# Turning O, K, Q and the softmax weights of the first layer by 32x32 transposes on VectorE and a round trip through DRAM

## The chip, the core and the metric

The kernel runs on one core of a Trainium2 chip. The core's engines are TensorE (PE, with its weight loads PEld), VectorE (DVE), ScalarE (ACT), GpSimd (POOL) and SyncE (SP); transfers are carried by 16 DMA engines and are issued from the queues of SP, ACT and POOL. The metric is the device time of one execution in microseconds; lower is better.

## What is computed

Two layers of a hybrid block work on 256 tokens (x) and 256 context tokens (ctx), with 1024 features. Each layer projects the normed tokens by one wide matrix, runs three branches (A: an mLSTM over 4 heads; B: differential attention over 8 heads, two per group; C: a Fourier mix), gates them and merges them by matrix products. The second layer produces x alone. Branch B and the merge, which the change touches:

```python
def attend(q, k, v, lam):
    s = jnp.einsum('bhmqd,bhmkd->bhmqk', q, k, preferred_element_type=jnp.float32) * (B_QK ** -0.5)
    p = jax.nn.softmax(s, axis=-1)
    w = p[:, :, 0] - lam * p[:, :, 1]
    return jnp.einsum('bhqk,bhkv->bhqv', w.astype(v.dtype), v)

def diffattn_out(o, subln_w, lam_init):
    return (rmsnorm(o, subln_w) * (1.0 - lam_init)).transpose(0, 2, 1, 3).reshape(bsz, n, B_WIDTH)
...
    y_b = diffattn_out(o_b, subln_w, lam_init) * jax.nn.silu(bz)
...
    y = g_a * (y_a @ w_a_out) + g_b * (y_b @ w_b_out) + g_c * (y_c @ w_c_out)
    return y @ w_out
```

## The kernel before

All products are made at float32 accuracy from fp32r halves: a matrix is split into a high part (a rounding copy on ScalarE) and a low part (a subtraction on VectorE), and `three` (line 591 on) issues three matmuls for each product. The main stream is a chain of such matmuls into banks named pm. Weights come in pieces of 512 rows by 256 columns: SP loads `raw` (4 buffers), ACT and DVE split it into `wh` and `wl` (3 buffers each), and TensorE uses a piece for 24 or more main matmuls.

Beside the main stream run side generators: `a_side`, `b_side`, `c_side` and a few more. Each is a Python generator that emits a few instructions and then yields the time at which its next step may be emitted. A planner, the class `Clocks`, books every instruction that is emitted with an estimated cost, and `tick` lets up to 5 side generators emit steps between two main matmuls when the planner's TensorE clock has reached the time that they yielded. So the planner's costs set the order of the instructions on every engine, and each engine then runs its own list strictly in order, held back by semaphores alone. A transfer that POOL issues is booked with 1040 ns of POOL, its bytes at 290 GB/s on one queue, and 2000 ns until it is seen; `when` adds 400 ns (READY_NS).

The order of the first layer's units is ORDER0: A0 to A3 are the mLSTM heads, B0 to B3 the attention groups (two heads each), C0 to C3 the Fourier groups, then the merges M0 (branch A), M2 (C), M1 (B) and the output W0. M1 comes last; with AHEAD its four gate products run first, then the side work of branch B is drained, then the products with B's result start. When M1 starts, two generators for the next adaLN rows start too; they load w_ada in pieces of 512 KB by 24 transfers on POOL's queue (tiles `adaw`).

In `b_side` (line 964 on) the tokens lie on the partitions. For each head TensorE turns K and Q by `nc.tensor.transpose` (`transpose`, line 234) into a side bank `ps`, four 128x128 blocks each, and ACT and DVE split them into kT and qT. Then come 8 items for each group (two heads times four blocks of queries): the score matmuls, the softmax (`softmax`), the turning of its weighted difference `Pt` on TensorE into `ps` (`w_transpose`: 2 blocks for the context queries, 4 for the others), its split into `W`, and the product with V (`pv`). An item's weights are turned LAG = 3 items after its scores. At the end O is normed, turned by TensorE (8 blocks for each group), and multiplied into the gate `Gb`.

Tiles of up to 4128 bytes for each partition come from one pool `g` with NGEN = 28 slots, taken in turn: a new tile waits until the readers of the one 28 before it are done.

The trace names the helper's line: L232 is a matmul, L236 a TensorE transpose, L161 anything of the other engines.

Of the kernel before, what the change touches and what calls it, by code (L numbers as in the profile page):

```python
# [27 lines left out]
NGEN = 28  # L28
# [13 lines left out]
ORDER1 = "A0 B0 A1 B1 A2 A3 C0 B2 B3 M0 C1 C2 C3 M1 M2 W0"  # L42
AHEAD = ((0, 1, 1), (1, 1, 0))
# [47 lines left out]
class Clocks:  # L91
    """When each engine gets to what is emitted, estimated, to place the side work among the main products."""
# [5 lines left out]
    def book(self, engine, outs, ins, cost, tail):  # L98
        """an instruction of engine: names of tiles written and read, time held, time until the result is seen"""
# [16 lines left out]
    def rotate(self, tag, bufs, name):  # L116
        """the tile called name takes the place of the one bufs before it"""
# [9 lines left out]
class Paced:  # L127
    """An engine whose instructions are booked as they are emitted."""
# [38 lines left out]
def hybrid_kernel(ctx: ExitStack, tc: tile.TileContext, t):  # L167
# [18 lines left out]
    def when(*tiles, banks=1):  # L186
        """the time at which the tiles are written and side banks are free"""
# [17 lines left out]
    def gen_pair(shape, name):  # L205
        """hi and lo parts, in one slot where they fit"""
# [39 lines left out]
    # ------------------------------------------------------------- constants  # L246
# [73 lines left out]
    def rstd_of(ss, n, shape):  # L320
        """(ss / n + eps) ** -0.5 on GpSimd, in place; returns the time at which it is done"""
# [4 lines left out]
    # ------------------------------------------------------------- per-layer small parameters  # L326
# [46 lines left out]
    def ada_rows(l, piece, dma):  # L373
        """w_ada of 512 columns"""
# [8 lines left out]
    def ada_mm(raws, brow, dst):  # L383
        """sc @ w_ada + b_ada: partitions 32 g + stream hold four partial sums"""
# [13 lines left out]
    def ada_finish(l, pc, ks=slice(0, 8)):  # L398
        """pc: shift and scale of some blocks of features"""
# [9 lines left out]
    def ada_gen(l, pieces):  # L409
        """shift and scale columns (pieces 0..3) as a side generator"""  # L410
# [34 lines left out]
    # ------------------------------------------------------------- norm -> feature-major h  # L445
# [3 lines left out]
    def norm_stats(tiles):  # L449
        """normalized copies of some token tiles"""  # L450
# [10 lines left out]
    def norm_apply(l, i, src, base):  # L461
        """src: the normalized transposed blocks base .. base + 3 of token tile i; returns the closing step"""
# [23 lines left out]
    # ------------------------------------------------------------- weight pieces  # L486
# [74 lines left out]
    def fm_chunk(rhs, evac, ntok, bank=ps_main, step=4):  # L561
        """two 128-column blocks of W, feature-major: out[block][128 cols, tokens]"""
# [24 lines left out]
    def tm_chunk(lhs, tiles, evac, single=False, step=4):  # L587
        """256 columns of W, token-major: out[pair][128 tokens, 2, 256]"""
# [24 lines left out]
    # ------------------------------------------------------------- side machinery  # L613
# [4 lines left out]
    def launch(g):  # L618
        rec = {"g": g, "due": 0.0, "done": False}
        side.append(rec)  # L620
        return rec
# [8 lines left out]
    def tick():  # L630
        pe0 = clocks["pe"]
        for rec in list(side[:ACTIVE]):
# [12 lines left out]

    def hrhs(t0, n):
# [7 lines left out]
    # ============================================================= one layer  # L654
    def layer(l, P):
# [8 lines left out]
        def packed(name, i):  # L664
            """[128, 2, NTOK], two of them in a slot where they fit"""
# [6 lines left out]
        # ---------- branch A: gates  # L672
        def gates_side():
            """kind x head i of the gate preactivations: from column 32 x + i, token-major, to a partition"""
# [71 lines left out]
        # ---------- branch A: heads  # L746
# [72 lines left out]
        def a_side(h):  # L819
# [97 lines left out]
            for dh in range(2):  # L917
# [9 lines left out]
        # ---------- branch B  # L927
# [58 lines left out]
        def b_side(g):  # L986
# [25 lines left out]

            def qk_transpose(X, nt, n, name):
                ps = ps_side()
                for i in range(nt):
                    transpose(ps[:, 128 * i:128 * i + 128], X[:, i, 128 * hd:128 * hd + 128], ident)
                T = gen([128, 2, n], F32R, name)
# [6 lines left out]
            def softmax(hd, i, p2, n):  # L1024
                """the weighted difference of both maps, short of the first one's 1 / sum"""
# [8 lines left out]
                for m_ in range(2):  # L1034
# [12 lines left out]
            def w_transpose(Pt, n):  # L1047
                ps = ps_side()
                for k in range(n // 128):
                    transpose(ps[:, 128 * k:128 * k + 128], Pt[:, 0, 128 * k:128 * k + 128], ident)  # L1050
                W = gen([128, 2, 512], F32R, "W")
# [18 lines left out]
            for it in items + [None] * LAG:  # L1070
                cur = None
                if it is not None and it[1] == 0:
                    hd = it[0]
                    kT = qk_transpose(K, 4, 512, "kT")
# [8 lines left out]
                if it is not None:  # L1083
# [13 lines left out]
                    pend.append((hd, i, Pt, at, n, ri[:, 0:1]))  # L1097
# [10 lines left out]
            for hd in range(2):  # L1108
# [8 lines left out]
        # ---------- branch C  # L1117
        def c_proj(g):
# [3 lines left out]
            def evu(a, pr, ps):  # L1122
                """sums and differences of features d and d + 128"""
# [64 lines left out]
        # ---------- merge  # L1188
        yacc = {}

        def merge(recs, ahead, key, first, final):
            ys = {}

            def split_y(q):
                ys[q] = gen_pair([128, 2, NTOK], "y")
# [300 lines left out]
```

## Time and profile before

| | |
|---|---|
| median of 3 runs | 1522.9 us (1522.81 to 1523.61) |
| span of the profiled execution, first to last instruction | 1521.1 us |
| PE busy | 1499.1 us (99%) |
| PEld busy | 1350.8 us (89%) |
| DVE busy | 971.5 us (64%) |
| ACT busy | 735.0 us (48%) |
| POOL busy | 145.7 us (10%) |
| granted TensorE clock, mean | 1.000 |

The page gives no other time of the profiled execution than its span, which is 1.8 us under the median of the runs. Busy time of TensorE counts pipelined matmuls from start to modelled end, so what a matmul costs is read from the distance between the starts of two that follow each other. The first layer's branch B lies between 350 and 800 us.

### The profile page before, as it was taken

How to read it: one execution, taken by the hardware profiler on the slowest of the kernel's cores; microseconds unless marked ns; L12 is line 12 of the kernel's file. 1: busy time of each engine (PE TensorE's matmuls, PEld its weight loads, DVE VectorE, ACT ScalarE, POOL GpSimd, SP SyncE). 2: the span in 40 equal slices, each digit the busy share in tenths (PEclk: the TensorE clock that was granted, in tenths of full speed). 3: DMA queues.
4: the chain of work that ended last, by engine and by line, in shares of the span. 5: the costliest groups of instructions: out<-in, count | busy, mean ns of one | idle time of the engine just before them, and what ended most of it. 6: DMA issues, size and time to landing. Idle time of an engine off the chain costs nothing.

```text
span 1521.1 us, 25867 instructions
## 1 busy us (share of the span) xinstructions
PE 1499.1 (99%) x10410; PEld 1350.8 (89%) x10410; DVE 971.5 (64%) x1833; ACT 735.0 (48%) x1384; POOL 145.7 (10%) x193
## 2 busy tenths in 40 slices
PE   6999999999999999999999999999999999999999
PEld 4888889999998987897786789999999999999998
DVE  3447666677677586436664367677687666977765
ACT  4443556544544545334432235545557554656443
POOL 4001000020100010001024001001020011000200
PEclk9999999999999999999999999999999999999999
DMA  9524333332222222223249337544344523545754
GB/s 310 167 84 127 87 94 105 105 97 70 75 67 69 70 84 70 84 84 97 70 144 337 78 112 228 139 131 133 115 111 118 167 84 109 169 139 153 256 162 151
DMA packets 181611, 192.07 MB, mean 126 GB/s; under 512 B 9818, under 2 KB 174612, under 8 KB 181492
## 3 DMA queue, kind: packets, MB, share of 16 engines
q1 hardware_dynamic: 170080, 159.93, 35.6%
q0 software_dynamic: 7936, 27.27, 5.9%
q10 hardware_dynamic: 3476, 3.23, 0.7%
q8 instruction: 81, 1.33, 0.4%
q14 instruction: 38, 0.31, 0.1%
HBM read 188.23 MB, written 2.17 MB: 125 GB/s over the span
## 4 chain that ended last, share of the span: by engine, by line
PE 92%; DVE 3%; SPq 2%; issue 1%; ACT 1%; DMA 1%; ACTq 0%; DVEq 0%
PE pm L232 76%; PE ps L232 13%; PE ps L236 3%; SPq L161 2%; DVE wl L161 1%; DVE Rx L161 1%; DMA raw<-in_w_in_dram 0%; DVE Rc L161 0%; DMA prow<-in_a_norm_w_dram 0%; DVE lfm L161 0%; DVE at L161 0%; ACT lse L161 0%; DVE Ga L161 0%; ACT wh L161 0%; DVE ntmp L161 0%
## 5 line engine op out<-in xcount | busy, mean ns | idle before, releaser
L161 DVE TENSOR_TENSOR wl<-raw,wh 128x1024 fp32r<-128x1024 f32 x280 | 340.9, 1223 | 193.4 <-ACT wh L161 192.8
L161 ACT CAST wh<-raw 128x1024 fp32r<-128x1024 f32 x280 | 293.6, 1054 | 169.0 <-PE pm L232 135.0
L232 PE MATMUL pm<-hTh,wh 128*128 128x256 f32 (+1 forms) x1008 | 349.0, 346 | 0.0
L232 PE MATMUL pm<-hTl,wh 128*128 128x256 f32 (+1 forms) x1008 | 342.8, 340 | 0.0
L232 PE MATMUL pm<-hTh,wl 128*128 128x256 f32 (+1 forms) x1008 | 342.4, 340 | 0.0
L232 PE MATMUL pm<-wh,hTh 128*128 128x256 f32 (+1 forms) x1152 | 329.8, 286 | 1.5 <-DVE Ga L161 0.8
L232 PE MATMUL pm<-wl,hTh 128*128 128x256 f32 (+1 forms) x1152 | 324.1, 281 | 0.7 <-DVE wl L161 0.7
L232 PE MATMUL pm<-wh,hTl 128*128 128x256 f32 (+1 forms) x1152 | 324.2, 281 | 0.3 <-DVE hTl L161 0.2
L232 PEld LDWEIGHTS pm<-wh,hTh 128*128 128x128 f32 x1152 | 217.3, 189 | 10.4 <-issue 5.5
L232 PEld LDWEIGHTS pm<-wl,hTh 128*128 128x128 f32 x1152 | 216.9, 188 | 2.1 <-DVE wl L161 1.0
L232 PEld LDWEIGHTS pm<-wh,hTl 128*128 128x128 f32 x1152 | 217.5, 189 | 0.7 <-DVE hTl L161 0.7
L232 PEld LDWEIGHTS pm<-hTh,wh 128*128 128x128 f32 x1008 | 189.7, 188 | 30.8 <-issue 9.9
L232 PEld LDWEIGHTS pm<-hTh,wl 128*128 128x128 f32 x1008 | 189.5, 188 | 23.3
L232 PEld LDWEIGHTS pm<-hTl,wh 128*128 128x128 f32 x1008 | 189.7, 188 | 19.0
L232 PE MATMUL pm<-y,wh 128*128 128x512 f32 (+1 forms) x768 | 192.7, 342 | 0.0
L232 PEld LDWEIGHTS pm<-y,wh 128*128 128x128 f32 x768 | 128.9, 188 | 18.3 <-issue 2.6
L232 PE MATMUL pm<-y,wl 128*128 128x512 f32 (+1 forms) x384 | 129.4, 337 | 0.0
L161 ACT ACTIVATE Pt<-ps,mx,qsc 128x512 f32<-128x512 f32 (+1 forms) x96 | 67.1, 706 | 27.7 <-DVE mx L161 22.0
L232 PEld LDWEIGHTS pm<-y,wl 128*128 128x128 f32 x384 | 72.2, 188 | 8.6
L232 PE MATMUL pm<-wh,yf 128*128 128x256 f32 x384 | 73.0, 287 | 0.0
L232 PEld LDWEIGHTS pm<-wh,yf 128*128 128x128 f32 x384 | 59.9, 188 | 0.3
L161 DVE TENSOR_REDUCE mx<-ps 128x1 f32<-128x512 f32 (+1 forms) x96 | 53.0, 593 | 4.3 <-PE ps L232 4.2
(243 smaller groups left out, 1969.8 us busy)
## 6 DMA issues: line engine op xcount, KB each, us to landing
raw<-in_w_in_dram SPq DMA_DIRECT2D x192, 512.0 KB, 3.7
adaw<-in_w_ada_dram POOLq DMA_DIRECT2D x32, 512.0 KB, 7.1
raw<-in_w_out_dram SPq DMA_DIRECT2D x24, 512.0 KB, 4.5
adaw<-in_w_ada_dram SPq DMA_DIRECT2D x16, 512.0 KB, 8.5
raw<-in_w_in_dram SPq DMA_DIRECT2D x32, 256.0 KB, 3.3
raw<-in_w_a_out_dram SPq DMA_DIRECT2D x16, 512.0 KB, 3.4
raw<-in_w_c_out_dram SPq DMA_DIRECT2D x32, 256.0 KB, 3.4
raw<-in_w_b_out_dram SPq DMA_DIRECT2D x16, 512.0 KB, 3.8
```

The costliest lines, as they stand in the source:

```text
L161: return f(*a, **k)
L232: nc.tensor.matmul(out=o, lhsT=a, rhs=b, start=start, stop=stop)
L236: nc.tensor.transpose(o, a, idn)
```

## The change

In the first layer, and there for branch B alone (FLIP_O, FLIP_K and FLIP_W are (1, 0), FLIP_H is (0, 0)), the turns leave TensorE. `flip_out` transposes 32x32 blocks on DVE into a tile and writes the tile to DRAM; `flip_in` reads it back with the 32x32 blocks exchanged, so that the whole is turned. Both transfers are issued from POOL's queue. The read takes 4 runs for each partition, of 512 bytes for K, Q and the 512-wide weights, 256 bytes for the 256-wide ones and 1 KB for O. K and Q of both heads go out together; the second head's are read back later. W and kT, qT are split from the turned tile in SBUF instead of from a PSUM bank. O's way back is a generator of its own (`tail`) that is always served, ahead of the five others; the scale of the norm (slcol) moves from the gate into the split of y in `merge`. In addition the pool has 31 slots instead of 28, and the scratch that the program keeps for POOL's transfers is set to 4096 (`dynamic_dma_scratch_size`). TensorE transposes of H, and of everything in the second layer, stay.

```diff
-NGEN = 28
+NGEN = 31
+FLIP_H, FLIP_O, FLIP_K, FLIP_W = (0, 0), (1, 0), (1, 0), (1, 0)
+FLIPB = 12
...
+    def flip_out(src, b):
+        groups = src.shape[1]
+        b = b.rearrange("p (b g j) -> p b g j", b=4, j=32)
+        vector.transpose(out=b.rearrange("p b g j -> p g b j"), in_=src.rearrange("p g (i b) -> p g b i", b=4))
+        d = dp.tile([128, 128 * groups], F32, tag="flip", name=nm("flip"), bufs=FLIPB)
+        gpsimd.dma_start(out=d, in_=b.rearrange("p b g j -> p (b g j)"))
+        return d
+    def flip_in(d, r):
+        gpsimd.dma_start(out=r.rearrange("p (a n) -> p a n", a=4), in_=d.rearrange("(a i) (b n) -> (i b) a n", a=4, b=4))
...
+            flips, loads = [], {}
+            if FLIP_K[l]:
+                for hd in range(2):
+                    b = gen([128, 1024], F32, "qkf")
+                    c = slice(128 * hd, 128 * hd + 128)
+                    flips.append(((flip_out(K[:, :, c], b[:, 0:512]), flip_out(Q[:, :, c], b[:, 512:512 + NTOK])), b))
+                yield when(*flips[0][0])
+                loads[0] = qk_load(0)
...
+                if FLIP_W[l]:
+                    return (flip_out(Pt[:, 0, 0:n].rearrange("p (g f) -> p g f", f=128), Pt[:, 1, 0:n]), Pt), ri, 0
...
+                for p in pend[:-1] if it is not None else pend:
+                    if FLIP_W[l] and not p[3]:
+                        d, Pt = p[2]
+                        yield when(d, banks=0)
+                        flip_in(d, Pt[:, 0, 0:p[4]])
...
+            if FLIP_O[l]:
+                s["tail"] = launch(tail(s, "yb", g, ov), True)
+                return
...
-    nc = bacc.Bacc("TRN2", target_bir_lowering=False, num_devices=1)
+    nc = bacc.Bacc("TRN2", target_bir_lowering=False, num_devices=1, dynamic_dma_scratch_size=4096)
```

Three places show what the change does to the order. On TensorE, in group B0, after the product of one item with V (ps from vt and W), before:

```order
L232 MATMUL ps_4097<-vt_2643,W_4007 128x256
L232 MATMUL ps_4097<-vt_2643,W_4007 128x128
L236 MATMUL ps_4106<-first_74,Pt_3864 128x128 x4
L232 MATMUL pm_3986<-wh_3848,hTh 128x256
L232 MATMUL pm_3986<-wl_3849,hTh 128x256
L232 MATMUL pm_3986<-wh_3848,hTl 128x256
```

and at such a place now:

```order
L234 MATMUL ps_4416<-vt_2643,W_4290 128x256
L234 MATMUL ps_4416<-vt_2643,W_4290 128x128
L234 MATMUL pm_4352<-hTh,wh_4248 128x512
L234 MATMUL pm_4352<-hTl,wh_4248 128x512
L234 MATMUL pm_4352<-hTh,wl_4249 128x512
```

The four transposes of the next item's Pt are gone, and the main stream follows at once. On DVE, in the softmax of an item of B0 (ri is the reciprocal sums, mx the maxima of the next item, W the low part of an earlier item's weights), before:

```order
L161 RECIPROCAL ri_3884<-ll_3865 128x2
L161 SCALAR_TENSOR_TENSOR ri_3884<-ri_3884,ll_3865,nlam_3133 128x1
L161 SCALAR_TENSOR_TENSOR Pt_3864<-Pt_3864,ri_3884 128x512
L161 TENSOR_TENSOR W_3891<-ps_3888,W_3891 128x256
L161 TENSOR_REDUCE mx_3908<-ps_3894 128x1
```

and now:

```order
L163 SCALAR_TENSOR_TENSOR ri_4011<-ri_4011,ll_3992,nlam_3133 128x1
L163 SCALAR_TENSOR_TENSOR Pt_3991<-Pt_3991,ri_4011 128x512
L163 STREAM_TRANSPOSE Pt_3991<-Pt_3991 128x4x4x32
L163 TENSOR_TENSOR W_4033<-Pt_3861,W_4033 128x256
L163 TENSOR_REDUCE mx_4053<-ps_4039 128x1
```

DVE has one instruction more for each item, and W's subtraction now reads what a transfer has brought back. On POOL, at the end of B3, where M1's gates run (os is the norm of O, brow a bias row of adaLN), before:

```order
L161 TENSOR_SCALAR os_7180<-os_7180 128x8
L161 TENSOR_TENSOR os_7180<-os_7180,chalf_87 128x8
L161 DMA adaw_7986<-in_w_ada_dram 128x2x512
L161 DMA adaw_7988<-in_w_ada_dram 128x2x512
L161 DMA adaw_7990<-in_w_ada_dram 128x2x512
L161 DMA adaw_7992<-in_w_ada_dram 128x2x512
L161 MEMSET brow_7994 128x1024
L161 DMA brow_7994<-in_b_ada_dram 2x1024
```

and now:

```order
L163 DMA adaw_8080<-in_w_ada_dram 128x2x512
L163 TENSOR_SCALAR os_7239<-os_7239 128x8
L163 TENSOR_TENSOR os_7239<-os_7239,chalf_87 128x8
L163 DMA flip_8205<-ybT_8203 128x1024
L163 DMA adaw_8216<-in_w_ada_dram 128x2x512
L163 DMA adaw_8218<-in_w_ada_dram 128x2x512
L163 DMA adaw_8220<-in_w_ada_dram 128x2x512
L163 DMA adaw_8222<-in_w_ada_dram 128x2x512
L163 MEMSET brow_8224 128x1024
L163 DMA brow_8224<-in_b_ada_dram 2x1024
L163 DMA ybT_8203<-flip_8205 128x4x256
```

Before, the norm of B3's O came ahead of all 24 loads of w_ada; now 16 of them stand ahead of it, and four more between the write of O and its read. The list of TensorE's main matmuls is the same in both, 8208 of them; in the second layer the side matmuls also stand at the same places among them.

## Rows read from the trace of the kernel before

**Rows 1.** The page's head, busy times by engine, TensorE's clock in 40 slices.

```profile
span 1521.1 us, 25867 instructions
...
PE 1499.1 (99%) x10410; PEld 1350.8 (89%) x10410; DVE 971.5 (64%) x1833; ACT 735.0 (48%) x1384; POOL 145.7 (10%) x193
...
PEclk9999999999999999999999999999999999999999
```

**Rows 2.** Waits of TensorE, whole span: total us, times, longest us.

```profile
PE ps L236 <- DMA crow<-in_c_dram: 7.6, 1, 7.6
PE ps L232 <- DMA adaw<-in_w_ada_dram: 2.8, 2, 2.5
```

**Rows 3.** TensorE transposes, 340 to 800 us: duration ns, first and last start.

```profile
L236 PE MATMUL ps<-first,Pt x96: 270/272/293, 382.9 to 779.9; 128*128 128x128 f32 x96
...
L236 PE MATMUL ps<-first,K x32: 270/272/291, 356.2 to 735.9; 128*128 128x128 f32 x32
...
L236 PE MATMUL ps<-first,Q x32: 270/272/275, 356.7 to 739.2; 128*128 128x128 f32 x32
...
L236 PE MATMUL ps<-first,O x32: 270/272/273, 464.8 to 792.1; 128*128 128x128 f32 x32
```

**Rows 4.** Timeline of TensorE, three places: start us, length us, instruction.

```profile
356.25 0.60 PE L236 MATMUL ps<-first,K 128*128 128x128 f32 x4
356.68 0.60 PE L236 MATMUL ps<-first,Q 128*128 128x128 f32 x4
357.04 0.36 PE L232 MATMUL pm<-wh,hTh 128*128 128x256 f32 x1
...
400.05 0.61 PE L236 MATMUL ps<-first,Pt 128*128 128x128 f32 x4
400.42 0.36 PE L232 MATMUL pm<-wh,hTh 128*128 128x256 f32 x1
400.63 0.27 PE L232 MATMUL pm<-wl,hTh 128*128 128x256 f32 x1
400.74 0.28 PE L232 MATMUL pm<-wh,hTl 128*128 128x256 f32 x1
...
791.39 1.03 PE L236 MATMUL ps<-first,O 128*128 128x128 f32 x8
792.18 0.72 PE L232 MATMUL pm<-y,wh 128*128 128x512 f32 x2
```

**Rows 5.** Busy us of PE, PEld, DVE, ACT, POOL; clock, DMA share, GB/s.

```profile
350.00:800.00 450.00, 450.00 (x2792) 388.88 (x2791) 281.52 (x525) 206.19 (x434) 35.46 (x33) 1.00 0.28 83
```

**Rows 6.** Groups by line, DVE: count, busy us, mean ns, idle before.

```profile
L161 DVE TENSOR_TENSOR K<-K,rtmp 128x512 f32<-128x512 f32 x8 | 5.5, 689 | 0.2
...
L161 DVE TENSOR_TENSOR_SCAN Rx<-cones,Rc,lfm 32x256 f32<-32x256 f32 x8 | 5.9, 740 | 0.3
...
L161 DVE TENSOR_SCALAR junk<-xn,nss 128x1024 f32<-128x1024 f32 x4 | 3.0, 754 | 2.9 <-POOL nss L161 2.9
```

**Rows 7.** Transfers issued by POOL: count, KB each, median us to landing.

```profile
adaw<-in_w_ada_dram POOLq DMA_DIRECT2D x32, 512.0 KB, 7.1
...
Rb<-dR POOLq DMA_DIRECT2D x16, 448.0 KB, 5.3
Rb<-dR POOLq DMA_DIRECT2D x8, 192.0 KB, 4.0
...
xmid<-xn POOLq DMA_DIRECT2D x8, 128.0 KB, 3.9
```

**Rows 8.** Groups by line, POOL: transfers' issue, mean ns of one.

```profile
L161 POOL DMA_DIRECT2D adaw<-in_w_ada_dram x32 | 23.3, 730 | 19.2 <-PE ps L232 11.3 <-ACT YQ L161 3.2 <-PE pm L232 2.4
L161 POOL DMA_DIRECT2D Rb<-dR x24 | 13.5, 564 | 1.8 <-PE ps L232 1.6
```

**Rows 9.** Timeline of POOL, the first loads for M1: start us, length us.

```profile
787.74 2.96 POOL L161 DMA_DIRECT2D adaw<-in_w_ada_dram  x4
...
817.26 2.88 POOL L161 DMA_DIRECT2D adaw<-in_w_ada_dram  x4 [6.17 <-PE ps L232]
```

More of the change, by code (lines that the diff above doesn't have):

```diff
@@ L244, in split, with flip, split_turned, gated @@
             vector.scalar_tensor_tensor(lo, src, scale, f32(hi), op0=ALU.mult, op1=ALU.subtract)
+    def flip_out(src, b):
[7 more added lines that the diff above has]
+        gpsimd.dma_start(out=r.rearrange("p (a n) -> p a n", a=4), in_=d.rearrange("(a i) (b n) -> (i b) a n", a=4, b=4))
+    def flip(src, name):
+        r = gen([128, 128 * src.shape[1]], F32, name)
+        d = flip_out(src, r)
+        yield when(d)
+        flip_in(d, r)
+        yield when(r)
+        return r
+    def split_turned(r, T):
+        split(r.rearrange("p (a g j) -> p g a j", a=4, j=32), *(T[:, z].rearrange("p (g a j) -> p g a j", a=4, j=32)
+                                                              for z in range(2)))
+    def gated(T, G):
+        t4 = T.rearrange("p (a i h j) -> p h i a j", a=4, h=2, j=32)
+        for h in range(2):
+            g = G[:, h, :].rearrange("p (i a j) -> p i a j", a=4, j=32)
+            vector.tensor_tensor(g, t4[:, h], g, op=ALU.mult)
+            yield 0
     xt = {}
@@ L616, in hybrid_kernel, with launch @@
     backlog = [0.0]
-    def launch(g):
-        rec = {"g": g, "due": 0.0, "done": False}
-        side.append(rec)
+    def launch(g, tail=False):
+        rec = {"g": g, "due": 0.0, "done": False, "tail": tail}
+        side.insert(0 if tail else len(side), rec)
         return rec
@@ L631, in tick @@
         pe0 = clocks["pe"]
-        for rec in list(side[:ACTIVE]):
+        tails = [r for r in side if r["tail"]]
+        for rec in tails + [r for r in side if not r["tail"]][:ACTIVE]:
             while not rec["done"] and rec["due"] <= clocks["pe"] < pe0 + SIDE_NS and \
@@ L644, in drain, with drain_all @@
                 step(r)
+    def drain_all(states):
+        for s in states:
+            drain([s["rec"]])
+            drain([s["tail"]] if "tail" in s else [])
     def hrhs(t0, n):
@@ L670, in packed, with tail @@
             return ST["half", name][:, 2 * (i % 2):2 * (i % 2) + 2, :]
+        def tail(s, key, g, src):
+            T = yield from flip(src, key + "T")
+            yield from gated(T, s["G"])
+            ST[key][g] = s["G"]
         def gates_side():
@@ L916, in a_side @@
             yield when(H)
-            for dh in range(2):
+            if FLIP_H[l]:
+                s["tail"] = launch(tail(s, "ya", h, H[:, i0:4, :].rearrange("p i (h f) -> p (i h) f", h=2)), True)
+                return
+            for dh in range(0 if FLIP_H[l] else 2):
                 ps = ps_side()
@@ L1073, in b_side @@
                     hd = it[0]
+                    if FLIP_K[l]:
+                        yield when(loads[hd])
                     kT = qk_transpose(K, 4, 512, "kT")
@@ L1096, in b_side @@
                     Pt, ri, at = yield from softmax(hd, i, p2, n)
-                    pend.append((hd, i, Pt, at, n, ri[:, 0:1]))
+                    pend.append([hd, i, Pt, at, n, ri[:, 0:1]])
+                    if FLIP_K[l] and (hd, i) == (0, NTL - 2):
+                        loads[1] = qk_load(1)
+                for p in pend[:-1] if it is not None else pend:
[3 more added lines that the diff above has]
+                        flip_in(d, Pt[:, 0, 0:p[4]])
+                        p[2], p[3] = Pt, when(Pt, banks=0)
                 if cur is not None:
@@ L1107, in b_side @@
             yield when(O)
-            for hd in range(2):
+            if FLIP_O[l]:
+                s["tail"] = launch(tail(s, "yb", g, ov), True)
+                return
+            for hd in range(0 if FLIP_O[l] else 2):
                 ps = ps_side()
@@ L1189, in layer, with merge @@
         yacc = {}
-        def merge(recs, ahead, key, first, final):
+        def merge(states, ahead, key, first, final):
             ys = {}
             def split_y(q):
-                ys[q] = gen_pair([128, 2, NTOK], "y")
-                split(ST[key].pop(q), ys[q][0], ys[q][1])
+                yh, yl = ys[q] = gen_pair([128, 2, NTOK], "y")
+                y = ST[key].pop(q)
+                if key == "ya" and FLIP_H[l]:
+                    for u in range(2):
+                        b = 8 * l + 2 * q + u
+                        split(y[:, u, :], yh[:, u, :], yl[:, u, :], scale=awcol[:, b:b + 1])
+                elif key == "yb" and FLIP_O[l]:
+                    split(y, yh, yl, scale=slcol[:, l:l + 1])
+                else:
+                    split(y, yh, yl)
             def spread(g, every):
@@ L1429, in do @@
         elif kind == "M":
-            recs = [ST[("a", "b", "c")[i], g]["rec"] for g in range(4)]
+            states = [ST[("a", "b", "c")[i], g] for g in range(4)]
             mo = [j for k, j in order[l] if k == "M"]
-            run(L["merge"](recs, AHEAD[l][i], ("ya", "yb", "yc")[i], mo.index(i) == 0, mo.index(i) == 2))
+            run(L["merge"](states, AHEAD[l][i], ("ya", "yb", "yc")[i], mo.index(i) == 0, mo.index(i) == 2))
         else:
```

18 lines of the change are left out of this document (15 added, 3 removed).

## The prediction

> **What bounds the kernel now.** I read the page's head first: TensorE is busy 1499.1 us of a span of 1521.1, and its clock stands at full speed in all forty slices, so no stretch of it can be had back from the clock [rows 1]. The waits of TensorE come next: the longest is one of 7.6 us at the start, the next group 2.8 us [rows 2]. So TensorE is the bound, everywhere, and what the change takes off its list comes off the time as long as no new wait appears. Then I read the stretch in which the edits lie, branch B of the first layer, 350 to 800 us: TensorE 450.0 of 450.0 us, VectorE 281.5 (63%), ScalarE 206.2 (46%), GpSimd 35.5 (8%), DMA engines 0.28 of their time at 83 GB/s [rows 5]. All that the change adds goes to VectorE, GpSimd and the DMA engines, the three that have room there. So two questions decide: what 192 transposes really cost TensorE, and whether what comes back from DRAM comes in time.
>
> **Removed from TensorE.** The transposes of Pt, K, Q and O are 96 + 32 + 32 + 32 = 192 [rows 3]. Their duration is 272 ns each, but a duration overlaps the neighbours; what they cost is the distance of the starts. K and Q of a head: eight, from 356.25 to the next main matmul at 357.04, so 0.79 us, 0.099 each. Four of a Pt: 400.05 to 400.42, 0.37, 0.0925 each. Eight of O: 791.39 to 792.18, 0.79 [rows 4]. 192 times 0.0925 to 0.099 is 17.8 to 19.0 us. Behind a group the first main matmul is also slow: 400.42 to 400.63 is 0.21 us, the next 0.11 [rows 4]. That is 0.1 us for each group. There are 32 items and 8 heads, and O's transposes come in four turns of eight: 44 groups, up to 4.4 us if each pays it once, half of it if half do. The sum is 18.8 + 2.2 = **21 us**, bounds 17.8 and 23.4.
>
> The Trainium skill, page "TensorE: Matmul & The Clock Gate", section "Part 4: PE-mode transpose", gives about 275 ns for a transpose in one kernel. By that figure 192 would give 53 us. The duration here agrees, at 272 ns, but the starts are 0.09 to 0.10 us apart [rows 3, 4], so the measurement decides for 19.
>
> **Added to VectorE.** For each of the four groups: K 2, Q 2, the weights 8 (four of 512 columns, four of 256) and O 1 (1024 columns), 13 transposes, 52 in all, which is the work of 48 of 128x512. No row shows this instruction. The nearest is an elementwise step of that shape from SBUF, 0.689 us; lower bound, half of a one-source 128x1024, 0.754 / 2 = 0.38; upper bound, the slowest elementwise form, the scan, 740 ns for 256 columns, 1.48 for 512 [rows 6]. So 48 times 0.689 = 33 us, bounds 18 and 71. I take 33: same shape, same memory, same engine. The splits of W, kT and qT change their source from PSUM to SBUF and are as many as before, and the gate's four products for each group take the place of steps of the same number and size; those I cost at nothing, since VectorE is idle 168 of the 450 us. VectorE rises from 281.5 to about 315 us, over some 430 us 73%, at the upper bound 82%. That is still beside TensorE, not on the path, unless it is bunched: VectorE runs in order, and the transposes stand inside the softmax chain of each item, which is needed three items later.
>
> **Added to GpSimd and the DMA engines.** 52 writes and 52 reads back. Rb's load costs GpSimd 0.564 us, adaw's 0.730, which brings two runs to each partition [rows 8]; so a run adds some 0.166, and a read of four runs is an estimate of 0.564 + 3 x 0.166 = 1.06. 52 x (0.564 + 1.06) = 84 us: GpSimd goes from 8% to about 28%. The bounds, 0.564 and four times that for a read, give 59 and 147 us, which still fits. A transfer of 128 to 448 KB lands 3.9 to 5.3 us after its issue, one of 512 KB 7.1 [rows 7]; K, Q and the wide weights are 256 KB, so about 4.3 us each way, O is 512 KB, so 5.3 to 7.1. The planner books 256 KB with 1.04 + 0.90 + 2.0 + 0.4 = 4.3 us, the same, so it places the readers about right. 25 MB more over 430 us are 58 GB/s beside 83; at the share of 0.28 for 83 the DMA engines come to some 0.48.
>
> For the weights there is room. The 32 items follow one another, from the first Pt at 382.9 to the last at 779.9, at a mean of 12.4 us [rows 3], and the weights of an item are used three items after its softmax: some 37 us for a way of about 4.3 + 4.3. At a cost of nothing, hidden by main matmuls, I therefore enter all items but the last ones of a group, K and Q (which also have other units' products around them), and the 31 slots, since no row shows a wait for a slot.
>
> **The end of B3.** Here the cover is thin. By the order, 111 main matmuls of 512 columns stand between the last product with V of B3 and the first product that takes its y, and two groups of eight adaLN matmuls. A 256-column one takes 0.11 us [rows 4], so 512 columns 0.22: (111 + 16) x 0.22 = 28 us. What must fit in: some five VectorE steps on O and the gate of 0.7 to 1.5 us (about 5 to 7 us), the norm's two small steps on GpSimd (1 to 2), O's write (5.3 to 7.1), its read (5.3 to 7.1), and between them four adaw loads that now stand in GpSimd's queue, 2.9 us [rows 9]. The sixteen adaw loads now ahead of the norm are waits by slot as well: one group of them waited 6.17 us for TensorE [rows 9], and the read of O stands behind a wait of that kind. The sum is 19.5 to 26 us without that wait, up to 32 with it. Against 28 us, a stall of 0 to 4; I enter **2 us**. The ends of B0 to B2 are far from M1 and cost nothing.
>
> **The sum.** The profiled execution has a span of 1521.1, 1.8 us under the median of 1522.9, and I take that distance as unchanged: 1521.1 - 21 + 2 + 1.8 = 1503.9, and since the 21 us rests on half of the slow followers, I say **1503**. That is 1.3% faster.
>
> **Rivals.**
> *The gain is halved at two places.* The tail of B3 takes 6 us and not 2, and GpSimd's queue is late for some of the last items of a group, 16 of them (four in each) by 0.3 us, 5 us more: 1522.9 - 21 + 11 = 1513. A rule of the chip could do it: GpSimd's issues might be held up by VectorE. Were each held for one VectorE instruction, up to 0.75 us [rows 6], 104 x 0.75 = 78 us more on GpSimd, near half busy, and six issues in B3's tail 4.5 us: 1522.9 - 21 + 6.5 = 1508 at the least. Against it, GpSimd's issues take 0.564 to 0.730 us while VectorE is 63% busy [rows 5, 8].
> The Trainium skill, page "SBUF — State Buffer", section "SBUF: two separate sides", says that GpSimd can't write the descriptors of its transfers while VectorE holds the port they share, and tells of an issue that went from 620 to 3100 ns. The means in rows 8 show nothing of it here.
>
> *Slower: read-backs come late at each use.* The split of W, kT or qT waits for a transfer while it stands at the head of ScalarE's and VectorE's lists; behind it stand the splits of the weight pieces, so TensorE waits for the main stream too. There are 32 + 8 + 4 = 44 such arrivals; the gain is gone at 21 / 44 = 0.48 us of lateness each, past all cover, and one that is 1 us late each time gives 1522.9 - 21 + 44 = 1546. It would come from GpSimd's single queue: writes wait there for VectorE, and the reads behind them, in order; the smaller scratch for its transfers might hold an issue back as well. Against it: 37 us of room at the mean against 9, and GpSimd under 30%.
>
> *No change.* Lateness of just 0.4 to 0.55 us for each arrival, or the upper price of VectorE's transposes with bursts in each softmax: 1520 to 1526.
>
> *More than forecast.* If TensorE were freed by the duration of a transpose and not by the distance of starts, 192 x 0.272 = 52 us: 1471. Rows 4 speak against it.
>
> **How the numbers follow.** The forecast, 1497 to 1508 (bounds of the transposes 17.8 to 23.4, tail 0 to 4, and some us of small waits): 0.62. Gain in part, 1508 to 1519: 0.16. No change: 0.06. Slower, 1526 and up: 0.14. Under 1497: 0.02. A measurement of this kernel tells some 0.2%, 3 us, from no change. So faster 0.80, same 0.06, slower 0.14. The range takes the first two cases, 1497 to 1519, which hold 0.78.
>
> **What would show it.** TensorE's list without the 192 transposes, its idle time still some 22 us in all (1521.1 - 1499.1), its clock at 1.00, and its busy time about 21 us less: right. Waits of TensorE on W, kT or on pieces (wl) in branch B: the slower rival. A wait for y near the first products with B's result in M1: the tail, with its price. VectorE's transposes at 0.4 to 0.7 us for 128x512, a share near 73% in the stretch; GpSimd's writes near 0.56 and reads near 1.06 us, landing after 4 to 5: the costs of the middle parts. The second layer should take as long as before. The prediction is wrong if the main matmuls themselves become slower, which nothing here shows.

## The result

The changed kernel takes 1504.7 us (median of 4 runs, 1502.67 to 1504.81), the kernel before 1523.2 beside it (1522.81 to 1523.61). The ratio is 0.9873, 95% interval 0.9859 to 0.9887: 18.5 us faster, where 1503 with a range of 1497 to 1519 was forecast. The profiled execution took 1504.65 us with a span of 1502.8. One execution of those below, the traced one of experiment 4, ran at a granted clock of 0.566 and took 2455.8 us; it is in no comparison.

Head of the page of the changed kernel, which answers to [rows 1]:

```profile
span 1502.8 us, 25788 instructions
...
PE 1482.4 (99%) x10218; PEld 1333.7 (89%) x10218; DVE 1018.2 (68%) x1885; ACT 736.6 (49%) x1384; POOL 215.1 (14%) x297
...
PEclk9999999999999999999999999999999999999999
```

Its row for the stretch of branch B, which answers to [rows 5] (us busy of TensorE, its loads, VectorE, ScalarE, GpSimd; clock, DMA share, GB/s):

```profile
350.00:780.00 430.00, 429.21 (x2584) 368.09 (x2584) 319.81 (x563) 202.30 (x417) 91.50 (x119) 1.00 0.44 134
```

TensorE has 192 instructions less in the whole kernel and is nearly as full as before in this stretch (429.21 of 430). VectorE went from 63% to 74% (319.81 of 430), GpSimd from 8% to 21%, the DMA engines from 0.28 to 0.44.

The order of the main matmuls is the same in both, so the start of the n-th of them can be compared:

| main matmul | before, us | after, us | difference |
|---|---|---|---|
| 1st | 23.2 | 24.4 | +1.2 |
| 1501st, ahead of branch B | 342.9 | 344.5 | +1.6 |
| 3985th, behind the first layer's merge | 903.7 | 885.7 | -18.0 |
| 6001st | 1204.0 | 1186.0 | -18.0 |
| 8101st | 1503.5 | 1485.4 | -18.2 |

The first layer's branch B and its merge brought 19.6 us. The start of the kernel lost 1.6. The change isn't what loses it: experiments 6, 7 and 11, which hold the whole change, reach the 1501st main matmul at 342.4 to 342.6 us in their traces, no later than the kernel without it at 342.9 (experiment 5 shows what differs). The second layer takes as long as before.

TensorE's waits in the first layer's branch B and merge of the changed kernel, 340 to 905 us, are these two (total, times, longest; those at the kernel's start are like [rows 2]); before there was none in that stretch:

```profile
PE ps L234 <- DVE kT L163: 0.6, 1, 0.6
PE ps L234 <- DVE qT L163: 0.2, 1, 0.2
```

They belong to one place, the second head of B0, here in TensorE's timeline:

```profile
411.93 0.28 PE L234 MATMUL pm<-wh,hTl 128*128 128x256 f32 x1
412.14 0.38 PE L234 MATMUL ps<-kT,qT 64*128 64x256 f32 x2
413.07 0.38 PE L234 MATMUL ps<-kT,qT 64*128 64x256 f32 x2 [0.55 <-DVE kT L163]
413.67 0.39 PE L234 MATMUL ps<-kT,qT 64*128 64x256 f32 x2 [0.22 <-DVE qT L163]
413.99 0.39 PE L234 MATMUL pm<-wh,hTh 128*128 128x256 f32 x1
```

The six score matmuls take 1.85 us from 412.14 to 413.99; those of the other 256-column items take 0.55 or 0.56, and one more is slow, at 623.3 us with 0.83. So this place costs 1.3 us and the other 0.3. K and Q had landed at 403.3 and 404.1 us; what was late were their splits on VectorE.

The added instructions, by form: VectorE's transposes (busy us, mean ns),

```profile
L163 DVE STREAM_TRANSPOSE Pt<-Pt 128x512 f32<-128x512 f32 x16 | 17.5, 1094 | 0.6
L163 DVE STREAM_TRANSPOSE Pt<-Pt 128x256 f32<-128x256 f32 x16 | 10.2, 636 | 0.6
L163 DVE STREAM_TRANSPOSE qkf<-K 128x512 f32<-128x512 f32 x8 | 8.6, 1080 | 0.0
```

GpSimd's issues, as in [rows 8] (32 writes and 16 of the 52 reads),

```profile
L163 POOL DMA_DIRECT2D flip<-Pt x32 | 18.1, 566 | 243.7 <-DVE O L163 73.2 <-issue 65.5 <-ACT wh L163 23.7
L163 POOL DMA_DIRECT2D qkf<-flip x16 | 12.2, 764 | 0.2 <-PE pm L234 0.2
```

and some of the transfers, as in [rows 7] (KB each, median us to landing):

```profile
flip<-Pt POOLq DMA_DIRECT2D x16, 256.0 KB, 2.3
Pt<-flip POOLq DMA_DIRECT2D x16, 256.0 KB, 3.3
qkf<-flip POOLq DMA_DIRECT2D x16, 256.0 KB, 4.8
ybT<-flip POOLq DMA_DIRECT2D x4, 512.0 KB, 4.8
```

A transpose of 128x512 takes 1.09 us, 1.6 times the elementwise step that stood for it [rows 6]. A write's issue costs 0.57 us, a read's 0.76; the first is as forecast, the second less than the 1.06 of the estimate. At the median a write of 256 KB lands after 2.3 us, a read of it after 3.3 (weights) or 4.8 (K and Q); O's 512 KB take 3.3 and 4.8.

How close the arrivals are is in the trace too: from the landing of each read to the start of the split that takes it there are, for the 32 weights, 0.7 to 19.5 us (median 6.2), for the 8 heads' K and Q 3.3 to 9.1. ScalarE, which takes them first, has no wait on such a transfer. At the end of B3 VectorE does wait: there the read of O needs 7.1 us to land. GpSimd's and then VectorE's timeline there:

```profile
823.18 0.63 POOL L163 DMA_DIRECT2D flip<-ybT  x1 [6.50 <-DVE ybT L163]
823.81 2.85 POOL L163 DMA_DIRECT2D adaw<-in_w_ada_dram  x4
...
828.46 0.78 POOL L163 DMA_DIRECT2D ybT<-flip  x1
```

```profile
835.64 1.29 DVE L163 TENSOR_TENSOR Gb<-ybT,Gb 128x512 f32<-128x512 f32 x2 [3.86 <-DMA ybT<-flip]
836.85 1.22 DVE L163 TENSOR_TENSOR wl<-raw,wh 128x1024 fp32r<-128x1024 f32 x1
838.15 1.28 DVE L163 SCALAR_TENSOR_TENSOR y<-Gb,slcol,y 128x1024 fp32r<-128x1024 f32 x1
```

y of B3 is ready at 839.4 us, and TensorE takes it first at 843.99: 4.6 us of room, and VectorE's 3.86 us of waiting, with wl of the next piece behind it, cost nothing.

### The profile page after: what moved, and what is told of

Read it like the earlier page. It is cut to its first block, busy times and chain, and to the rows that moved or that the text cites. A ratio compares the mean times of both kernels' runs of the same rounds, so it can differ in the third digit from the quotient of the medians.

```text
span 1502.8 us, 25788 instructions
## 1 busy us (share of the span) xinstructions
PE 1482.4 (99%) x10218; PEld 1333.7 (89%) x10218; DVE 1018.2 (68%) x1885; ACT 736.6 (49%) x1384; POOL 215.1 (14%) x297
## 4 chain that ended last, share of the span: by engine, by line
PE 91%; DVE 4%; SPq 2%; ACT 1%; issue 1%; DMA 1%; ACTq 0%; DVEq 0%
PE pm L234 76%; PE ps L234 13%; SPq L163 2%; PE ps L238 1%; DVE wl L163 1%; DVE Rx L163 1%; DVE Rc L163 0%; ACT wh L163 0%; DMA raw<-in_w_in_dram 0%; DMA prow<-in_a_norm_w_dram 0%; DVE lfm L163 0%; DVE at L163 0%; ACT lse L163 0%; DVE Ga L163 0%; DVE ntmp L163 0%
## 5 line engine op out<-in xcount | busy, mean ns | idle before, releaser
L234 PE MATMUL pm<-wl,yf 128*128 128x256 f32 x192 | 53.9, 281 | 0.0
```

What stands on the lines that cost most here:

```text
L234: nc.tensor.matmul(out=o, lhsT=a, rhs=b, start=start, stop=stop)
```

## The experiments

**1 to 3. One part alone.** One flag each:

```diff
-FLIP_H, FLIP_O, FLIP_K, FLIP_W = (0, 0), (1, 0), (1, 0), (1, 0)
+FLIP_H, FLIP_O, FLIP_K, FLIP_W = (0, 0), (1, 0), (0, 0), (0, 0)
```

and (0, 0), (1, 0), (0, 0) for K and Q, (0, 0), (0, 0), (1, 0) for the weights.

> The changed kernel with O alone turned by VectorE and DRAM; K, Q and the weights go back to TensorE; 31 slots. Theory (what counts is the distance of the transposes' starts, and the new work is hidden): 32 transposes less, 3.2 us by the starts that the trace of before shows for O, and up to 0.4 us of slowed followers, so 3.2 to 3.6 us under before: about 1520. Rival (O's way back at the end of B3 stalls the merge, some us): 1521 to 1525, with a wait of TensorE near the first products with B's result. If the slots or the scratch cost 1.3 us at the start, all are that much later.

> The changed kernel with K and Q alone turned by VectorE and DRAM; 31 slots. Theory: 64 transposes less, 6.2 us by the starts, and 0.2 to 0.8 us of followers, less up to 1.3 us where a split of kT stands late on VectorE: 5 to 7 us under before, 1516 to 1518. Rival (each head's K and Q come late, 8 arrivals): a gain under 4 us, with TensorE's waits on kT and qT adding up to over 3 us.

> The changed kernel with the softmax weights alone turned by VectorE and DRAM; 31 slots. Theory: 96 transposes less, 9.4 us by the starts, and 1 to 2 us of followers: 9.5 to 11.5 us under before, 1512 to 1514. Rival (32 arrivals come late by some tenths of a us): 3 to 8 us under before. The three parts alone add up to 18 to 21 us under the theory; if they share a late queue, they add up to clearly more than the 18.5 us of the whole change.

Measured against 1523.2: O alone 1518.5 (ratio 0.9968, 0.9956 to 0.9981), K and Q alone 1516.0 (0.9948, 0.9935 to 0.9962), the weights alone 1512.7 (0.9926, 0.9913 to 0.9938). The medians hold the start, which differs from execution to execution. Between the 1501st and the 6001st main matmul the parts bring 3.9, 7.2 and 10.9 us, together 22.0, the whole change 19.5. The starts of their transposes in the trace of before give 3.2, 6.2 and 9.4, together 18.8; the rest is slowed followers, 0.7 + 1.0 + 1.5. So each part is worth its starts and a little more, and the rivals of late arrivals are out: no part gains less, and none alone has a wait of TensorE between 340 and 905 us. Together they give back 2.5 us. Adding up the distances of starts by kind of matmul, before and after, shows where: the transposes bring 18.8 us in the whole change too, the main matmuls start 2.3 us closer in all (0.9 less than the followers of the three parts), and the score matmuls of 256 columns lose 1.6, which is 1.3 at 412 us and 0.3 at 623.

**4. The slots and the scratch alone.**

```diff
-NGEN = 28
+NGEN = 31
...
-    nc = bacc.Bacc("TRN2", target_bir_lowering=False, num_devices=1)
+    nc = bacc.Bacc("TRN2", target_bir_lowering=False, num_devices=1, dynamic_dma_scratch_size=4096)
```

> The kernel before with 31 slots and the scratch of 4096 and nothing else of the change. Theory (the slow start of TensorE in the profile of the changed kernel, 1.2 us at its first main matmul, has to do with neither): 1523.2, within 0.5 us of before, first main matmul at 23.2 us. Rival (slots or scratch cause it): about 1524.5, first main matmul near 24.4 us.

Measured: 1523.0 against 1523.2, ratio 0.9996 (0.9987 to 1.0005). Neither costs anything that the interval of -2.0 to 0.8 us lets see. The first main matmul, the other half of the expectation, isn't read from this run. What differs at the start is shown by experiment 5.

**5. The transfers left out.**

```diff
     def flip_out(src, b):
...
+        dry[0] = True
         gpsimd.dma_start(out=d, in_=b.rearrange("p b g j -> p (b g j)"))
+        dry[0] = False
...
-            return f(*a, **k)
+            return f(*a, **k) if not dry[0] else None
```

and the same around the read, so that the planner books them and the order stays.

> The changed kernel with every instruction in the same order, but its 104 transfers through DRAM are left out: the transposes on VectorE stay, and W, kT, qT and the gate are split from what they leave in SBUF (so the turned blocks don't change places). Theory (the transfers and GpSimd's issues are hidden, and the 1.3 us wait for kT and qT near 412 us is VectorE's backlog and not a transfer's): 1504 to 1505, and the wait near 412 us is still there. Rival (transfers cost the 1 to 3 us by which the parts alone add up to more than the whole): 1501 to 1503, without that wait.

Measured: 1502.8 (1502.73 to 1504.73; ratio 0.9867, 0.9853 to 0.988). The two differ by 1.97 us at the 1501st main matmul, by 1.88 at the 3985th and by 1.91 at the 6001st: in branch B and the merge, 104 transfers and 69 us of GpSimd cost TensorE less than 0.1 us. The wait at 412 us is there as in the changed kernel:

```profile
PE ps L237 <- DVE kT L166: 0.6, 1, 0.6
...
PE ps L237 <- DVE qT L166: 0.2, 1, 0.2
```

The theory's mechanism holds. The median fell into the rival's range, and the traced execution shows why for itself: it is ahead at the start, before any of the transfers. TensorE's timeline at the start of the changed kernel and of this one (start us, length us):

```profile
22.58 1.95 PE L238 MATMUL ps<-first,junk 128*128 128x128 f32 x8
...
25.71 0.41 PE L234 MATMUL pm<-wl,hTh 128*128 128x256 f32 x1
25.93 0.41 PE L234 MATMUL pm<-wh,hTl 128*128 128x256 f32 x1
```

```profile
21.11 1.07 PE L241 MATMUL ps<-first,junk 128*128 128x128 f32 x8
...
23.98 0.28 PE L237 MATMUL pm<-wl,hTh 128*128 128x256 f32 x1
24.10 0.28 PE L237 MATMUL pm<-wh,hTl 128*128 128x256 f32 x1
```

256 columns follow each other after 0.21 to 0.22 us in the one and 0.12 in the other: 1.2 and 2.1 columns for each ns. The first number is what the lower of the two levels, 1.2 GHz, would give at one column for each cycle, and the second lies above it; the column of the granted clock shows 1.00 in both, so the level is inferred from the starts. By them the changed kernel's profiled execution ran at the lower level until some 29 us, the other until some 20. Beside experiment 4 there are thirteen traces: three have the wide distance (the changed kernel, K and Q alone, and experiment 12) and reach the 1501st main matmul at 344.3 to 344.5 us, ten have the narrow one (the kernel before among them) and reach it at 342.4 to 342.9.

**6. Each transfer twice.** Second issues that the planner does not see:

```diff
         gpsimd.dma_start(out=d, in_=b.rearrange("p b g j -> p (b g j)"))
+        nc.gpsimd.dma_start(out=d, in_=b.rearrange("p b g j -> p (b g j)"))
```

and the same for the read.

> The changed kernel with the same order, but each of the 104 transfers is issued twice in a row, unseen by the planner: 69 us more of GpSimd's time, 25 MB more. A way through DRAM becomes longer by one write's and one read's issue, some 1.3 us, at K and Q more, since four pairs go together. Theory (room for the weights is tens of us): within 2 us of the changed kernel, 1503 to 1507, any new wait of TensorE standing at kT, qT or y of B3. Rival (each of 44 arrivals counts): 44 x 1.3 = 57 us more, 1562.

Measured: 1667.5 us (ratio 1.0942, 1.0921 to 1.0963), 163 us more than the changed kernel and above even the rival. The expectation had the delay wrong. The second issue writes the same tile, so it waits until the first has landed, and holds GpSimd's list meanwhile. GpSimd's timeline in this kernel at B0's first K and Q:

```profile
375.09 0.54 POOL L255 DMA_DIRECT2D flip<-qkf  x1 [4.16 <-DMA flip<-qkf]
375.62 0.77 POOL L163 DMA_DIRECT2D qkf<-flip  x1
379.21 0.76 POOL L261 DMA_DIRECT2D qkf<-flip  x1 [2.81 <-DMA qkf<-flip]
```

The waits of TensorE, then those of ScalarE (total, times, longest):

```profile
PE ps L234 <- ACT qT L163: 81.1, 8, 19.2
PE ps L234 <- ACT W L163: 29.4, 8, 12.7
```

```profile
ACT W L163 <- DMA Pt<-flip: 73.0, 20, 10.9
ACT kT L163 <- DMA qkf<-flip: 48.3, 6, 18.0
ACT qT L163 <- DMA qkf<-flip: 31.6, 8, 5.5
```

From the first write to the landing of Q this takes 29.5 us (357.8 to 387.3), in the changed kernel 10.1 (359.8 to 369.9): 19.4 us later. TensorE loses 15.1 us there. The difference, 4.3 us, is the room that the trace of the changed kernel gives that place (4.6 to 4.8). So the mechanism of the slower rival is real: at this place ScalarE stands with the split of a late tile at the head of its list, and TensorE follows, one for one, once the room is used.

**7. Each transpose of VectorE twice.**

```diff
         vector.transpose(out=b.rearrange("p b g j -> p g b j"), in_=src.rearrange("p g (i b) -> p g b i", b=4))
+        nc.vector.transpose(out=b.rearrange("p b g j -> p g b j"), in_=src.rearrange("p g (i b) -> p g b i", b=4))
```

> The changed kernel with the same order, but each of VectorE's 52 transposes is issued twice, unseen by the planner: 53 us more of VectorE's time (16 x 1.094 + 16 x 0.636 + 16 x 1.07 + 4 x 2.02). Theory (VectorE has room, 75% busy in the stretch before, 87% then): 0 to 6 us more than the changed kernel, 1504 to 1511, most of it at kT and qT. Rival (VectorE's time counts one for one, since its list is on the path): 53 us more, 1558.

Measured: 1528.1 us (ratio 1.0028, 1.0019 to 1.0038), 23 more than the changed kernel. Between the 1501st and the 6001st main matmul of its trace (of the fastest of nine runs, 1524.7 us) it is 22.2 us, for 53 us of VectorE: four tenths of the added time reach the path. Neither expectation holds. VectorE has no room for a second helping of this size, though it is busy just 363.9 of the 450 us from 350 to 800; it is late at kT, qT and W, in bursts. TensorE's waits on these:

```profile
PE ps L234 <- ACT qT L163: 6.4, 4, 3.3
...
PE ps L234 <- DVE kT L163: 2.5, 4, 1.0
PE ps L234 <- DVE qT L163: 1.9, 5, 1.1
PE ps L234 <- ACT W L163: 1.7, 2, 1.5
```

**8. The true cost in the planner.**

```diff
-                c.book("dve", on, rn, 68 + 60 * pointers + (2.1 if "scan" in name else 1.042) * n, 95)
+                c.book("dve", on, rn, 68 + 60 * pointers + (2.1 if "scan" in name or name == "transpose" else 1.042) * n, 95)
```

> The changed kernel with one number of the planner changed: a transpose on VectorE is booked with 2.1 ns for each column instead of 1.042, near the 1.09 us that one of 512 takes. Theory (the wait of 1.3 us for kT and qT comes from VectorE being later than the planner believed): that wait goes and nothing else comes, 1503 to 1504. Rival (the order has other places where the planner is wrong by as much): 1504 to 1506, with waits of the same size elsewhere.

Measured: 1510.0 us (ratio 0.9914, 0.99 to 0.9928), 5.3 more than the changed kernel. TensorE's waits for kT and qT are gone. That fits VectorE's lateness against the planner as their cause, as do experiments 5 (without transfers the wait stays) and 7 (with more of VectorE's time it grows); as the order moved too, this run doesn't show it by itself. B3 now ends later among the main matmuls, and its end has no room. GpSimd's, VectorE's and TensorE's timelines there:

```profile
840.09 0.76 POOL L163 DMA_DIRECT2D ybT<-flip  x1 [5.32 <-issue]
```

```profile
844.52 1.29 DVE L163 TENSOR_TENSOR Gb<-ybT,Gb 128x512 f32<-128x512 f32 x2 [10.63 <-DMA ybT<-flip]
```

```profile
841.64 0.39 PE L234 MATMUL pm<-y,wl 128*128 128x512 f32 x1
847.11 0.79 PE L234 MATMUL pm<-y,wh 128*128 128x512 f32 x1 [5.08 <-ACT y L163]
```

y's high part is there at 847.1 us and its low part at 848.4, 8.9 later than in the changed kernel, and TensorE waits 5.1 and 0.5. This is the tail that the prediction feared. The way from the last product with V to y isn't longer than in the changed kernel, 24 us (824.4 to 848.4) against 26; what shrank is its cover, 63 main matmuls between the two instead of 111. The waits cost more than their 5.6 us: from 849 to 853 us TensorE is granted 0.54 of its clock, and from the last main matmul ahead of the waits to the 3985th this kernel falls 7.5 us behind the changed one.

**9 and 10. The second layer as well.** (1, 1) for O, K and W, and for W alone.

> The changed kernel with the second layer's O, K, Q and weights turned by VectorE and DRAM as well. There 144 transposes cost TensorE 11.6 us by their starts in the changed kernel (Pt 5.93, K 2.92, Q and O 2.76). Theory (the second layer gives the work the same cover): 10 to 12 us under the changed kernel, 1492 to 1495. Rival (the second layer, with 256 tokens, has half the items between an item and its use, so arrivals come later than TensorE needs them; main matmuls are fewer around them too): no gain or slower, 1504 to 1530, with waits of TensorE on kT, qT, W or y between 1000 and 1300 us.

> The changed kernel with only the weights of the second layer turned by VectorE and DRAM as well, 64 transposes of 5.9 us. Theory: 5 to 7 us under the changed kernel, 1498 to 1500. Rival as for the whole second layer: no gain or slower; if this alone gains and the whole second layer doesn't, the fault is K's, Q's or O's way.

Measured: 1569.4 us (ratio 1.0302, 1.0288 to 1.0316) and 1519.9 (0.9977, 0.9967 to 0.9986): 65 and 15 us more than the changed kernel. The rival holds, but not by late arrivals in the middle: up to the 7201st main matmul both are ahead of the changed kernel, by 20.7 and 5.9 us counted from the 1501st (part of it side work that has been put off), and lose 85.9 and 22.4 us from there to the 7501st. There the last merge needs branch B, whose items are not done, and hardly any main matmul is left beside them. 1380 to 1420 us of the changed kernel and of the run with W alone, and 1380 to 1460 of the run with all (columns as above):

```profile
1380.00:1420.00 40.00, 40.00 (x343) 40.00 (x343) 27.23 (x48) 19.87 (x45) 8.56 (x12) 1.00 0.68 231
```

```profile
1380.00:1420.00 40.00, 28.48 (x186) 26.37 (x185) 21.27 (x41) 16.16 (x43) 11.46 (x17) 0.74 0.49 154
```

```profile
1380.00:1460.00 80.00, 28.32 (x112) 21.90 (x112) 32.67 (x63) 20.93 (x57) 17.37 (x26) 0.56 0.20 65
```

TensorE idles and, having idled, is granted 0.74 and 0.56 of its clock, so what is left runs slower too.

**11. The planner believes the transfers earlier.**

```diff
-                    c.wrote[o] = ("dma", c.t[q] + 2000)
+                    c.wrote[o] = ("dma", c.t[q] + (0 if any("flip" in v.name for v in tiles) else 2000))
```

> The changed kernel with one number of the planner changed: a transfer of a turn is booked as seen when its bytes are moved, 2.0 us earlier than before. What uses it is emitted earlier, up to 4 us for the two ways; the chip does the same. In the changed kernel the reads land 0.7 to 19.5 us (median 6.2) before the split of the weights and 3.3 to 9.1 us before those of K and Q. Theory (the hiding is bought by the planner's number; ScalarE and VectorE run in order, so a split that stands too early holds back the main stream): some 14 of 32 weights and some of K and Q come late by 1 to 3 us, and the time rises by 5 to 30 us, 1510 to 1535. Rival (there is room beyond it, since TensorE uses the split some us later): within 3 us of the changed kernel.

Measured: 1503.7 us (1503.4 to 1503.8; ratio 0.9869, 0.9854 to 0.9884). By its time the rival holds and the theory's 5 to 30 us fall, but the theory's mechanism shows at one place. Between the 1501st and the 6001st main matmul this kernel takes 1.1 us longer than the changed one; its traced execution is ahead by the start alone, 1.9 us at the 1501st. VectorE, at the head of its list, waits for the read of B1's O; the splits of the next K and Q stand behind that on ScalarE and VectorE, and TensorE waits for them. VectorE's and TensorE's timelines:

```profile
611.76 1.29 DVE L163 TENSOR_TENSOR Gb<-ybT,Gb 128x512 f32<-128x512 f32 x2 [2.20 <-DMA ybT<-flip]
```

```profile
620.23 0.59 PE L234 MATMUL ps<-kT,qT 64*128 64x256 f32 x4 [1.25 <-ACT qT L163]
621.04 0.38 PE L234 MATMUL ps<-kT,qT 64*128 64x256 f32 x2 [0.22 <-DVE qT L163]
```

The median room of the weights stayed (6.2 and now 6.3 us), that of K and Q went from 4.7 to 3.0. At the tightest places the room is gone: two of the weights and one head's K and Q are split within 0.1 us of their landing, where the least was 0.7 and 3.3. So at the median it is not the booked 2 us that hide the weights' way; the read is issued behind the next item's softmax and its tile is used an item or two later. At those tightest places the planner's number did hide it: the changed kernel has 1.4 to 4.7 us of room there.

**12. Two groups of the second layer.** W of its B0 and B1 alone:

```diff
+GROUPS_K, GROUPS_W = (4, 0), (4, 2)
...
-                if FLIP_W[l]:
+                if (g < GROUPS_W[l]):
```

> The changed kernel with the weights of the second layer's groups B0 and B1 turned by VectorE and DRAM as well (its B2 and B3, K, Q and O stay on TensorE): 32 transposes less, 3.0 us by their starts. Theory (the second layer lost at its end alone, where the last group's items were not done when the last merge needed them; in this order 12 side matmuls are left there, 10 in the changed kernel, 36 with all weights turned): 2 to 4 us under the changed kernel, 1500 to 1503, TensorE's clock at 1.00 throughout. Rival (it loses at any group): 1504 to 1510, with TensorE idle before the second layer's last merge and a lower granted clock there.

Measured: 1511.4 us (ratio 0.9923, 0.9909 to 0.9936), 6.7 more than the changed kernel. Both parts of the theory can be seen apart. At the 7201st main matmul it is 3.5 us ahead, the 3.0 of the transposes and a little more; from there to the 7451st it loses 11.0. The side work that was put off stands at the end, and O of the last group (in the second layer it lies in the tile Q) is turned right before the product that needs it. TensorE's timeline, and the row of the stretch:

```profile
1402.19 0.84 PE L235 MATMUL ps<-vt,W 128*128 128x256 f32 x6
1406.50 1.08 PE L239 MATMUL ps<-first,Q 128*128 128x128 f32 x4 [3.47 <-DVE Q L164]
```

```profile
1400.00:1420.00 20.00, 15.98 (x115) 15.47 (x114) 9.91 (x15) 6.92 (x13) 8.53 (x12) 0.83 0.72 255
```

How much of the 11.0 us is put-off work and how much waiting was not taken apart. No complete version here beats the changed kernel by more than the start's chance; whether the queues of SP or ACT would carry the turns better was not tried.

## Why the prediction was right, point by point

- **The bound.** TensorE at 99% with nothing but the transposes to give back: right. The 192 went, the clock stayed at 1.00, and idle time stayed near 20 us (1502.8 - 1482.4).
- **Removed from TensorE, 21 us by the distance of starts.** Right, term by term: in the whole change the transposes bring 18.8 us by their starts and the followers 2.3, where 18.8 and 2.2 were forecast. By the duration column it would have been 52 us, and none of the runs comes near. The Trainium skill's 275 ns for a transpose ("TensorE: Matmul & The Clock Gate", section "Part 4: PE-mode transpose") agrees with the duration in these traces, 272 ns [rows 3]. What the change gave back for each is 21.1 / 192 = 0.11 us with its share of the followers.
- **VectorE, 33 us of transposes.** The term was mis-sized: they took 53 (17.5 + 10.2 + 8.6 + 8.5 + 8.1), inside the bounds of 18 and 71. The nearest row by shape [rows 6] was a poor stand-in. That a share of up to 82% would still lie beside TensorE was too sure: at 74% it cost 1.3 us at one place, and a second 53 us, with VectorE at 81% (363.9 of 450), cost 22 (experiment 7).
- **GpSimd, 84 us.** 69, as a read of four runs costs 0.76 us and not 1.06. VectorE did not hold its issues back: of the 32 writes of Pt, 13 were issued with VectorE busy for over 80% of the issue and took 0.565 us, 11 with VectorE busy for under 20% and took 0.572. The prediction's comparison was weaker than it looks, since the issues of [rows 8] stand hardly anywhere in the stretch of [rows 5]: Rb's lie outside it, 16 of 24 between 130 and 280 us, where VectorE is busy 60% (90.58 of 150), and adaw's start 12 us before its end. The partial-gain rival by that mechanism finds nothing here. Nor does the Trainium skill's rule on the port ("SBUF — State Buffer", section "SBUF: two separate sides") show; it speaks of a VectorE instruction that holds the port, and whether those of this kernel do isn't shown.
- **Transfers, 4.3 us each way.** Writes of 256 KB 2.3, reads 3.3 to 4.8; hidden whole (experiment 5). The DMA engines came to 0.44 where 0.48 was forecast.
- **Room of 37 against 9 us for the weights.** The step was wrong, with no harm. From the issue of a write to the product that takes its weights it is 26 us at the mean (12.0 to 45.0), not 37, and the read goes out an item later than the write, 7.9 us after its landing at the median. What is left from landing to split is 0.7 to 19.5 us, for K and Q 3.3 to 9.1, and experiment 6 confirms 4.3 at one of them. The slower rival was nearer than its 0.14 let appear.
- **The end of B3, 2 us.** It cost nothing, with 4.6 us to spare. The sum of 19.5 to 26 us against 28 was right in kind, at its upper end: from 813.4, the last product with V, to 839.4 it took 26 us, and 30.6 were there. The 111 main matmuls were counted rightly, but the two groups of adaLN products hold 16 matmuls each and not 8. Experiment 8 shows the stall at 5.1 and 0.5 us when B3 ends later.
- **What was missing.** 1.6 us at the score matmuls of kT and qT, and the start, 1.6 us in the profiled execution. So 21.1 less 1.6 is the 19.5 between the 1501st and the 6001st main matmul; less 1.6 at the start, and with some tenths from elsewhere, it makes the 18.3 by which the spans differ. The forecast's 21 less 2 came to nearly the same by other items. That the term of 21 came out is the forecast's merit; that a stall of 2 us which didn't come stood in for losses which weren't forecast is luck.

## What to carry to other kernels

Price an instruction on a full, pipelined engine by the distance of starts with and without it, never by its duration. Work moved to idle engines is free only where its consumer has room: read the margin from landing to use, place by place, and look first at the ends, where a merge waits and little else is left to run; the same edit that paid in one layer cost 65 us in the next. An engine that runs its list in order can be late in bursts well under full share, so a share is no proof of room.

## What was not expected of the hardware

A 32x32 block transpose of VectorE on float32 takes 1.09 us for 128x512, 0.64 for 128x256 and 2.02 for 128x1024, 1.6 times an elementwise step of the first shape and some 1.8 ns for each further column ((2.02 - 0.64) / 768). At the median a write of 256 KB to DRAM was seen 2.3 us after its issue, a read of it in runs of 512 bytes after 3.3 to 4.8.

By the distance of its starts, TensorE ran at the lower of its two levels at the start, up to a point that differs between executions, 20 us in one and 29 in another; the traces of the two kinds lie some 2 us apart behind it. The column of the granted clock shows 1.00 in both. The runs of one kernel fall into two groups about as far apart (changed kernel 1502.67 and 1504.65 to 1504.81; without transfers 1502.73 to 1502.84 and 1504.73); that the runs without a trace differ for the same reason fits, and isn't shown.
